# Attention scores for two heads at once, with new cost estimates in the kernel's own ordering

## The chip, the cores and the metric

The kernel runs on one core of a Trainium2 chip. The metric is the device time of one execution in microseconds; a figure without a unit is in microseconds too. Engines: TensorE (PE in the profile; PEld is its weight load), VectorE (DVE), ScalarE (ACT), GpSimd (POOL) and SyncE (SP), which issues the transfers. SBUF is the on-chip memory; PSUM is where TensorE writes, eight banks here used as eight tiles of 128 × 512 numbers.

## What is computed

A block of 256 tokens of width 1024 goes through two blocks in a row. The first has three mixers side by side (a short convolution, a stick-breaking attention with eight heads of 64, a retention), then attention to a memory, then a two-layer net. The second has a state-space mixer, a gated net with a short convolution, an attention with eight heads, and such a net again, with a layer norm behind each. The last attention is the place of the change. For each head its scores are the sum of a product over 128 features and one over 64 rotary features, whose key is shared by all heads:

```
scores = (einsum('bqhd,bkhd->bhqk', qn, k_nope)
          + einsum('bqhr,bkr->bhqk', qr, k_rope)) * scale
scores = where(key_idx <= q_idx, scores, -inf)
p = softmax(scores);  out = einsum('bhqk,bkhd->bqhd', p, v)
```

## The kernel before

All tokens stay on the chip; the weights (about 226 MB) are streamed in chunks of up to 1 MB. Products are made at nearly full float32 precision from pairs: every weight chunk is copied to a rounded high part `wh` (a cast on ScalarE) and a low part `wl` (the difference on VectorE), the activations likewise (`ah`, `al`), and each product is three passes on TensorE: high·high, high·low, low·high (`mm3`, line 685). Smaller products, such as those of the attention, are single products of float32 operands (`mm1`, line 963); in the trace each of these is two records.

The program is written by a planner while it is built. Wrappers around the engines (`Lane`, `Plan`, lines 272 to 435) add up for every instruction when it would start and end: `cost` (line 353) estimates its duration, `LATE` (line 25) the time from one engine's end to another's start, and the transfers have a rate of their own (line 412). Work that isn't one of the large products is a generator, a task (`spawn`, line 655), that yields where it has to wait for an engine. After each group of large products the planner calls `tick` (line 619), which steps every task whose operands are there by the estimates. `split_next` (line 594) decides when the next half chunk is cast and subtracted: if it is late against the estimated need (`need`, line 602: the estimated TensorE time of all chunks prepared, from `UNIT` in line 28 and `sums` in line 486, less the `work` done, line 688, and `skew`), or if the engine would otherwise be idle soon. So the estimates set no wait, but the order of the instructions in each engine's queue. Each engine works through its queue in order. The next weight transfer is issued when the second half of a chunk has been subtracted (`pump`, line 490).

Norms stand between the layers: a root-mean-square norm before the memory attention, the first net and the second block, a layer norm after each layer of the second block (`rms` line 875, `layernorm` line 902). Behind each, the result is transposed on TensorE and split into high and low.

The last attention (`attention`, line 1784): keys `knT`, queries `qnT` for 128 features, `krT` and `qrT` for the 64 rotary ones. `krT` has the shared key twice, in partitions 0 to 63 and 64 to 127, and `qrT` has an even head in the lower and an odd head in the upper 64 partitions. The queries come in two halves of four heads (line 1969). After each, the task `head` (line 1924) is started for each of the four heads. It takes one of four small PSUM tiles `sm`, makes 128 × 384 scores (the first 128 queries see 128 keys, the others 256): two products of 128 rows, two that add the mask, two of 64 rows. Then VectorE reduces the maxima, ScalarE takes the exponential with its sum, VectorE normalises, TensorE transposes, ScalarE copies, TensorE multiplies by the values `v`, and the result is split into `oT`. The output projection `ao` takes two heads per chunk and calls `before` (line 1977) to wait for those it needs.

In the first mixer the task `stick` (line 1005) handles two heads of 64 features together:

```
zs = yield from self.sm.wait(2)
rs = (slice(0, 64), slice(64, 128))
for z, r in zip(zs, rs):
    self.mm1(z[:, 0:256], kT[r, pair, 0:128], qT[r, pair, :], True)
for z, r in zip(zs, rs):
    self.mm1(z[:, 256:384], kT[r, pair, 128:256], qT[r, pair, 128:256], False)
```

Of the kernel before, what the change touches and what calls it, by code (L numbers as in the profile page):

```python
# [8 lines left out]
BF16 = mybir.dt.bfloat16  # L9
# [15 lines left out]
LATE = {("pe", "act"): 0.2, ("pe", "dve"): 0.2, ("act", "pe"): 0.22, ("dve", "pe"): 0.15, ("pool", "dve"): 0.06,  # L25
        ("pool", "act"): 0.06, ("pool", "pe"): 0.05, ("act", "pool"): 0.18, ("dve", "pool"): 0.16, ("act", "act"): 0.15,
        ("pe", "pe"): 0.0, ("dma", "act"): 0.95, ("dma", "dve"): 0.95, ("dma", "pe"): 0.95, ("dma", "pool"): 0.95}
UNIT = 6 / 2400
AHEAD = 1.0
FILL = 0.8  # L30
SOON = 0.0
# [258 lines left out]
class Plan:  # L290
# [62 lines left out]
    def cost(self, kind, name, out, ins, args, kw):  # L353
        n = 1
        for s, c in out.ap[1:]:
            n *= c
        psum = any(x.space == PSUM for x in ins)
        aps = sum(1 for x in ins[1:] if x.free_size() == 1)
        if kind == "pe":
            if name == "transpose":  # L360
                return 0.11
            if kw["rhs"].dtype == F32:
                m = kw["lhsT"].shape[-1]
                return 4 * max(n, m) / 2400 * (0.53 if m <= 64 else 1.0)
            return (n if n >= 256 or kw["rhs"].dtype == BF16 else 4 * n) / 2400
        if kind == "act":
            t = n / 1200 + (0.05 if psum else 0.093)
            if name in ("activation", "mul"):
                t += 0.093 * (len(ins) - 1) + (0.093 if "accum_out" in kw else 0)
            return t  # L370
        if kind == "dve":
            for x in ins[:1]:
                m = 1
                for s, c in x.ap[1:]:
                    m *= c
                n = max(n, m)
            if name == "reciprocal":
                return n / 160 + 0.07
            fast = name in ("tensor_copy", "tensor_scalar", "tensor_scalar_mul", "tensor_scalar_add") and not psum
            return n / (1920 if fast else 960) + 0.068 + (0.06 * aps if "scalar" in name else 0)  # L380
        if kind == "pool":
            return (0.3 + 0.16 * n if n < 3 else 0.6) if name == "tensor_tensor" else n / (280 if name == "tensor_copy" else 960) + 0.11
        return 0.0
# [88 lines left out]
class Kern:  # L472
    def __init__(self, nc, tc, a, dbg=None):
# [11 lines left out]
        self.work = self.skew = 0.0  # L485
        self.sums = np.concatenate([[0.0], np.cumsum([len(ks) * max(n, P) * UNIT for _, ks, _, n, _ in self.plan])])

# [197 lines left out]
    def mm3(self, outs, lhs, rhs, first, last, weights=True):  # L685
        passes = ((0, 0), (0, 1), (1, 0))
        if weights:
            self.work += sum(o.free_size() for o in outs) * 3 / 2400
        for q, (i, j) in enumerate(passes):
            for n, o in enumerate(outs):  # L690
                self.nc.tensor.matmul(o, lhsT=lhs[i], rhs=rhs[j][n] if isinstance(rhs[j], list) else rhs[j],
                                      start=first and q == 0, stop=last and q == 2, skip_group_check=True)
# [27 lines left out]
    def xstat(self, tag, nks, lhs, blocks, tail=0, after=None, before=None):  # L720
# [29 lines left out]
        if tail:  # L750
            chs = []
            for tau in range(2):
# [3 lines left out]
                for c in range(tail):  # L756
# [19 lines left out]
                    else:  # L776
                        self.skew = 0.0 if c == tail - 1 else self.skew + nk * chs[c][0].shape[2] * UNIT / 2
                    self.tick()
        return ps

    def wmixed(self, tag, act, nk, consumers, tasks=None):
# [4 lines left out]
        for tau in range(2):  # L786
            for c in range(n):
# [8 lines left out]
                if tau == 0:  # L796
                    self.skew = 0.0 if c == n - 1 else self.skew + nk * wh.shape[2] * UNIT / 2
                if tau:
# [637 lines left out]
    def ssd(self, h, act):  # L1436
# [259 lines left out]
        for tau in range(2):  # L1696
            got = [0]
            for i, (half, c) in enumerate(last):
                ch = so(half, c, (tau,), chs[i] if tau else None)
                chs.append(ch)  # L1700
                if tau == 0:
                    self.skew = 0.0 if i == 2 else self.skew + 2048 * UNIT / 2
                if i:
# [80 lines left out]
    def attention(self, h, act):  # L1784
# [4 lines left out]
        krT = pool.tile([P, S], F32, tag="krT", name="krT")  # L1789
        knT = pool.tile([P, 8, S], F32, tag="knT", name="knT")  # L1790
        qnT = pool.tile([P, 8, S], F32, tag="qnT", name="qnT")
        qrT = pool.tile([P, 4, S], F32, tag="qrT", name="qrT")
# [7 lines left out]
        for n, o in (("kvn", 0), ("qn", 256)):  # L1800
            b, w = ROWS[n]
# [89 lines left out]
        for tau in range(2):  # L1891
            for tag, nk, src, blocks in (("qr", 3, cq, [(0, 512)]), ("v", 2, ckv, [(0, 512), (512, D)])):
# [12 lines left out]
                else:  # L1905
                    self.skew = nk * wh.shape[2] * UNIT / 2 if tag == "qr" else 0.0
                if tag == "qr":
# [5 lines left out]
        def evac_to(dst, h0=0):  # L1913
            def run(pt, t):
                nc.scalar.copy(dst[:, h0 + t:h0 + t + 2, :], pt.rearrange("p (a b) -> p a b", a=2))
                self.free(pt)
                yield
            return run
# [2 lines left out]
        scale = 192 ** -0.5  # L1921
        obank = {}

        def head(i):
            sc = yield from self.sm.wait()
            r = slice(64 * (i % 2), 64 * (i % 2) + 64)
            self.mm1(sc[:, 0:128], qnT[:, i, 0:128], knT[:, i, 0:128], True)
            self.mm1(sc[:, 128:384], qnT[:, i, 128:256], knT[:, i, :], False)
            self.mm1(sc[:, 0:128], self.identb, self.maskb, False)
            self.mm1(sc[:, 256:384], self.identb, self.maskb, False)  # L1930
            self.mm1(sc[:, 0:128], qrT[r, i // 2, 0:128], krT[r, 0:128], False)
            self.mm1(sc[:, 128:384], qrT[r, i // 2, 128:256], krT[r, :], False)
            yield "dve"
            mx = self.tiny.tile([P, 2], F32, tag="mx", name="mx")
            nc.vector.tensor_reduce(mx[:, 0:1], sc[:, 0:128], axis=AX.X, op=MAX)
            nc.vector.tensor_reduce(mx[:, 1:2], sc[:, 128:384], axis=AX.X, op=MAX)
            nc.vector.tensor_scalar_mul(mx, mx, -scale)
            p = yield from ps_.wait()
            sm = self.tiny.tile([P, 2], F32, tag="sm", name="sm")
            cuts = ((0, 128), (128, 384))  # L1940
            for t, (b, e) in enumerate(cuts):
                nc.scalar.activation(p[:, b:e], sc[:, b:e], AF.Exp, bias=mx[:, t:t + 1], scale=scale, accum_out=sm[:, t:t + 1])
            self.sm.put(sc)
            yield "dve"
            nc.vector.reciprocal(sm, sm)
            for t, (b, e) in enumerate(cuts):
                nc.vector.tensor_scalar_mul(p[:, b:e], p[:, b:e], sm[:, t:t + 1])
            yield
            pt = yield from self.sm.wait()
            for b in range(0, 384, P):  # L1950
                nc.tensor.transpose(pt[:, b:b + P], p[:, b:b + P], self.ident)
            ps_.put(p)
            yield "act"
            w = yield from pT.wait()
            nc.scalar.copy(w, pt[:, :384])
            self.sm.put(pt)
            yield
            po = yield from self.sm.wait()
            c = slice(P * i, P * i + P)
            self.mm1(po[:, 0:256], v[:, 0, c], w[:, 0:256], True)  # L1960
            self.mm1(po[:, 128:256], v[:, 1, c], w[:, 256:384], False)
            pT.put(w)
            yield "act"
            yield from self.split((oT[0][:, i, :], oT[1][:, i, :]), po[:, :256])
            self.sm.put(po)

        hs = []
        for b in (0, 4):
            self.wstat("qn", cq, 3, evac_to(qnT, b))
            self.until(*g_qr, *g_v)  # L1970
            for i in range(b, b + 4):
                hs.append(self.spawn(head(i)))
                self.tick()
        g_, b_ = self.bcast("lmg1", self.gb, "gb"), self.bcast("lmb1", self.gb, "gb")
        act = self.new_act()

        def before(c):
            self.until(*hs[:2 * c + 2])
        ps = self.xstat("ao", [2] * 4, self.lhs(oT), [(0, 512), (512, 1024)], tail=TAIL["ao"], before=before,
                        after=lambda t, p, got: self.layernorm(t, h, g_, b_, act, p, got))  # L1980
        close()
# [106 lines left out]
```

## Time and profile before

| | |
|---|---|
| time, median of 3 runs | 1233.27 us (1233.09 to 1234.08) |
| the profiled execution, its own time | 1233.43 us |
| its span, first to last instruction | 1231.7 us |
| instructions | 20769 |
| VectorE, ScalarE, GpSimd busy | 852.7, 718.0, 53.2 us |

The span is what the trace covers; the time has 1.7 us more around it. The busy time of an engine counts a stretch once however many of its instructions overlap. Starts of neighbouring TensorE records lie closer together than their durations, since they are pipelined, so the pace of TensorE is read from start to start. Nearly all instructions come from one helper, so the line (L284) tells nothing, and the names of the tiles tell what an instruction is: `sm<-krT,qrT` is a product of the rotary key and query into a small PSUM tile.

### The profile page before, as it was taken

What the parts mean: (1) busy time and instruction counts of PE and PEld (TensorE: products, weight loads), DVE (VectorE), ACT (ScalarE), POOL (GpSimd) and SP (SyncE); (2) the same over time, 40 slices, a digit from 0 to 9 for tenths busy, and PEclk for the clock granted to TensorE, in tenths of its full rate; (3) what the DMA queues carried; (4) which work ended last, traced back from release to release, by engine and by line L of the source; (5) the groups of instructions that cost most, each with busy time, mean ns of one, the idle gap of its engine ahead of it and who ended that gap; (6) DMA issues with size and microseconds to landing.
All of it is one profiled execution on the core that took longest, in us unless ns stands there. A gap on an engine that the chain in (4) does not pass through costs nothing.

```text
span 1231.7 us, 20769 instructions
## 1 busy us (share of the span) xinstructions
PE 1214.2 (99%) x8468; PEld 1109.8 (90%) x8468; DVE 852.7 (69%) x1378; ACT 718.0 (58%) x1181; POOL 53.2 (4%) x85
## 2 busy tenths in 40 slices
PE   7999999999999999999999999999999999999997
PEld 5979999989989998888999898999988888999986
DVE  5666848677747765446887797888855866888853
ACT  5666546446536554345789765666643665666631
POOL 0011000000000000000111201000000000000000
PEclk9999999999999999999999999999999999999999
DMA  7643355546444556524556545555673442455560
GB/s 257 246 159 132 142 198 221 185 163 227 172 154 167 211 193 226 183 105 172 224 206 237 190 172 197 180 185 193 216 262 105 164 184 106 171 206 190 209 251 34
DMA packets 35425, 227.71 MB, mean 185 GB/s; under 512 B 4321, under 2 KB 4993, under 8 KB 11522
## 3 DMA queue, kind: packets, MB, share of 16 engines
q1 hardware_dynamic: 35330, 226.39, 51.1%
q8 instruction: 66, 1.08, 0.3%
q14 instruction: 29, 0.24, 0.1%
HBM read 225.27 MB, written 1.10 MB: 184 GB/s over the span
## 4 chain that ended last, share of the span: by engine, by line
PE 93%; DVE 3%; DMA 1%; ACT 1%; issue 0%; POOL 0%; SPq 0%; POOLq 0%; DVEq 0%; ACTq 0%
PE mm L284 84%; PE sm L284 9%; DMA wr<-wts 1%; DVE wl L284 1%; DVE x L284 1%; DVE tk L284 0%; POOL rs L284 0%; ACT wh L284 0%; SPq L284 0%; DVE dtw L284 0%; DVE ln L284 0%; DVE al L284 0%; ACT L284 0%; ACT tk L284 0%; POOLq L2084 0%
## 5 line engine op out<-in xcount | busy, mean ns | idle before, releaser
L284 DVE TENSOR_TENSOR wl<-wr,wh 128x1024 fp32r<-128x1024 f32 (+3 forms) x408 | 478.7, 1196 | 174.2 <-ACT wh L284 173.5
L284 ACT CAST wh<-wr 128x1024 fp32r<-128x1024 f32 (+3 forms) x408 | 403.9, 1030 | 160.4 <-PE mm L284 88.6
L284 PE MATMUL mm<-ah,wh 128*128 128x256 f32 (+1 forms) x1496 | 417.1, 279 | 0.0
L284 PE MATMUL mm<-ah,wl 128*128 128x256 f32 (+1 forms) x1496 | 413.6, 276 | 0.1
L284 PE MATMUL mm<-al,wh 128*128 128x256 f32 (+1 forms) x1496 | 413.4, 276 | 0.0
L284 PEld LDWEIGHTS mm<-ah,wh 128*128 128x128 f32 (+1 forms) x1496 | 280.2, 187 | 1.6 <-issue 1.1
L284 PEld LDWEIGHTS mm<-al,wh 128*128 128x128 f32 (+1 forms) x1496 | 280.3, 187 | 0.4
L284 PEld LDWEIGHTS mm<-ah,wl 128*128 128x128 f32 (+1 forms) x1496 | 280.2, 187 | 0.4 <-DVE wl L284 0.3
L284 DVE SCALAR_TENSOR_TENSOR r<-mm,pcol,r 128x255 f32<-128x255 f32 (+2 forms) x212 | 86.9, 474 | 35.1 <-ACT r L284 35.1
L284 PE MATMUL mm<-wl,ah 128*128 128x512 f32 (+3 forms) x320 | 106.1, 338 | 3.0 <-DVE wl L284 2.9
L284 PE MATMUL mm<-wh,ah 128*128 128x512 f32 (+3 forms) x320 | 108.7, 346 | 0.0
L284 PE MATMUL mm<-wh,al 128*128 128x512 f32 (+3 forms) x320 | 106.3, 338 | 0.5 <-DVE al L284 0.5
L284 PE MATMUL mm<-wh,gTh 128*128 128x512 f32 x304 | 96.2, 391 | 0.0
L284 PE MATMUL mm<-wl,gTh 128*128 128x512 f32 x304 | 95.6, 389 | 0.0
L284 PE MATMUL mm<-wh,gTl 128*128 128x512 f32 x304 | 95.5, 389 | 0.0
L284 ACT ACTIVATE r<-mm,pcol 128x256 f32<-128x256 f32 x96 | 48.9, 560 | 43.3 <-PE mm L284 43.3
L284 PEld LDWEIGHTS mm<-wl,ah 128*128 128x128 f32 x320 | 60.4, 190 | 10.0 <-DVE wl L284 4.6
L284 PEld LDWEIGHTS mm<-wh,gTl 128*128 128x128 f32 x304 | 57.1, 188 | 11.9
L284 PEld LDWEIGHTS mm<-wl,gTh 128*128 128x128 f32 x304 | 57.1, 188 | 11.8
L284 PEld LDWEIGHTS mm<-wh,gTh 128*128 128x128 f32 x304 | 56.7, 188 | 12.0 <-issue 0.6
L284 PEld LDWEIGHTS mm<-wh,al 128*128 128x128 f32 x320 | 60.2, 189 | 7.0 <-DVE al L284 1.2
L284 PEld LDWEIGHTS mm<-wh,ah 128*128 128x128 f32 x320 | 60.3, 189 | 6.5 <-issue 0.7
(296 smaller groups left out, 1576.6 us busy)
## 6 DMA issues: line engine op xcount, KB each, us to landing
wr<-wts SPq DMA_DIRECT2D x186, 1024.0 KB, 4.8
wr<-wts SPq DMA_DIRECT2D x11, 768.0 KB, 4.3
gb<-prow SPq DMA_DIRECT2D x12, 512.0 KB, 6.5
dec<-rows SPq DMA_DIRECT2D x8, 768.0 KB, 8.1
wr<-wts SPq DMA_DIRECT2D x4, 704.0 KB, 4.1
wr<-wts SPq DMA_DIRECT2D x4, 512.0 KB, 6.5
tk<-mem SPq DMA_DIRECT2D x2, 512.0 KB, 7.3
out<-x SPq DMA_DIRECT2D x4, 256.0 KB, 2.1
```

The source lines that it names most:

```text
L284: r = f(*args, **kw)
```

## The change

The scores move from `head` to a new task `scores`, which takes two PSUM tiles, makes the 128-row products of two heads, then the masks of both, then the 64-row products of the two heads in turn, and starts a `head` task for the softmax of each. `before` waits for the pairs first, then for the heads. Beside that, the estimates change: large products cost 17/16 of their columns at 2.4 per nanosecond (also in `UNIT` and `work`), ScalarE 1/1110 us per column and 0.1 us, VectorE 0.11 us in place of 0.068 us per instruction.

```diff
-UNIT = 6 / 2400
+UNIT = 6 * 17 / 16 / 2400
...
-            return (n if n >= 256 or kw["rhs"].dtype == BF16 else 4 * n) / 2400
+            return (n * 17 / 16 if n >= 256 else n if kw["rhs"].dtype == BF16 else 4 * n) / 2400
         if kind == "act":
-            t = n / 1200 + (0.05 if psum else 0.093)
+            t = n / 1110 + 0.1
...
-            return n / (1920 if fast else 960) + 0.068 + (0.06 * aps if "scalar" in name else 0)
+            return n / (1920 if fast else 960) + 0.11 + (0.06 * aps if "scalar" in name else 0)
...
-            self.work += sum(o.free_size() for o in outs) * 3 / 2400
+            self.work += sum(o.free_size() for o in outs) * 3 * 17 / 16 / 2400
...
-        def head(i):
-            sc = yield from self.sm.wait()
-            r = slice(64 * (i % 2), 64 * (i % 2) + 64)
-            self.mm1(sc[:, 0:128], qnT[:, i, 0:128], knT[:, i, 0:128], True)
-            self.mm1(sc[:, 128:384], qnT[:, i, 128:256], knT[:, i, :], False)
-            self.mm1(sc[:, 0:128], self.identb, self.maskb, False)
-            self.mm1(sc[:, 256:384], self.identb, self.maskb, False)
-            self.mm1(sc[:, 0:128], qrT[r, i // 2, 0:128], krT[r, 0:128], False)
-            self.mm1(sc[:, 128:384], qrT[r, i // 2, 128:256], krT[r, :], False)
+        def scores(j):
+
+            scs = yield from self.sm.wait(2)
+            for e, sc in enumerate(scs):
+                i = 2 * j + e
+                self.mm1(sc[:, 0:128], qnT[:, i, 0:128], knT[:, i, 0:128], True)
+                self.mm1(sc[:, 128:384], qnT[:, i, 128:256], knT[:, i, :], False)
+            for sc in scs:
+                self.mm1(sc[:, 0:128], self.identb, self.maskb, False)
+                self.mm1(sc[:, 256:384], self.identb, self.maskb, False)
+            for q, k, o in ((slice(0, 128), slice(0, 128), slice(0, 128)), (slice(128, 256), slice(0, 256), slice(128, 384))):
+                for e, sc in enumerate(scs):
+                    r = slice(64 * e, 64 * e + 64)
+                    self.mm1(sc[:, o], qrT[r, j, q], krT[r, k], False)
+            for e, sc in enumerate(scs):
+                hs[2 * j + e] = self.spawn(head(2 * j + e, sc))
+
+        def head(i, sc):
             yield "dve"
...
-        hs = []
+        hs, pairs = {}, []
...
-            for i in range(b, b + 4):
-                hs.append(self.spawn(head(i)))
+            for j in range(b // 2, b // 2 + 2):
+                pairs.append(self.spawn(scores(j)))
                 self.tick()
...
-            self.until(*hs[:2 * c + 2])
+            self.until(*pairs[:c + 1])
+            self.until(*[hs[i] for i in range(2 * c + 2)])
```

## Rows read from the trace of the kernel before

**Rows 1.** The page: its span and TensorE's busy time with its share.
```profile
span 1231.7 us, 20769 instructions
PE 1214.2 (99%) x8468; PEld 1109.8 (90%) x8468; DVE 852.7 (69%) x1378; ACT 718.0 (58%) x1181; POOL 53.2 (4%) x85
```

**Rows 2.** Busy time by stretch: its length, PE, PEld, DVE, ACT, POOL, clock, DMA.
```profile
0.00:20.00 20.00, 13.48 (x42) 8.61 (x43) 10.75 (x24) 10.39 (x17) 1.57 (x7) 1.00 0.83 288
20.00:1223.00 1203.00, 1200.01 (x8425) 1100.96 (x8424) 837.87 (x1345) 705.54 (x1158) 50.74 (x77) 1.00 0.51 184
...
540.00:580.00 40.00, 39.42 (x245) 34.28 (x243) 22.27 (x42) 20.07 (x35) 1.10 (x2) 1.00 0.29 107
...
940.00:960.00 20.00, 18.62 (x100) 15.63 (x99) 15.51 (x26) 10.36 (x20) 1.88 (x2) 1.00 0.39 132
...
1030.00:1060.00 30.00, 29.27 (x210) 26.76 (x209) 22.65 (x37) 18.33 (x31) 1.87 (x2) 1.00 0.34 117
...
1223.00:1231.70 8.70, 0.71 (x4) 0.25 (x2) 4.11 (x11) 2.02 (x6) 0.93 (x1) 0.83 0.17 61
```

**Rows 3.** Timeline of TensorE in the last attention: start, duration, instructions merged.
```profile
989.88 0.82 PE L284 MATMUL sm<-knT,qnT 128*128 128x128 f32 x4
990.53 0.28 PE L284 MATMUL sm<-maskb,identb 128*128 128x128 bf16 x2
990.74 0.92 PE L284 MATMUL sm<-krT,qrT 64*128 64x128 f32 x4
...
991.59 0.92 PE L284 MATMUL sm<-knT,qnT 128*128 128x128 f32 x4
992.35 0.28 PE L284 MATMUL sm<-maskb,identb 128*128 128x128 bf16 x2
992.55 0.92 PE L284 MATMUL sm<-krT,qrT 64*128 64x128 f32 x4
993.40 0.38 PE L284 MATMUL sm<-knT,qnT 128*128 128x128 f32 x1
...
997.03 0.44 PE L284 MATMUL sm<-cst,p 128*128 128x128 f32 x2
```

**Rows 4.** Busy time by stretch inside the last attention; columns as in rows 2.
```profile
989.88:997.03 7.15, 7.15 (x43) 4.83 (x41) 4.99 (x14) 4.44 (x12) 0.00 (x0) 1.00 0.40 147
997.03:1005.25 8.22, 8.22 (x66) 8.00 (x66) 6.02 (x17) 7.53 (x20) 0.00 (x0) 1.00 0.01 3
1005.25:1012.39 7.14, 7.14 (x42) 4.83 (x40) 5.84 (x16) 4.35 (x15) 0.00 (x0) 1.00 0.70 255
```

**Rows 5.** Timeline of TensorE in the first mixer, around one pair of heads.
```profile
47.87 0.92 PE L284 MATMUL sm<-qT,kT 64*128 64x256 f32 x8
48.72 0.50 PE L284 MATMUL mm<-wh,ah 128*128 128x512 f32 x1
```

**Rows 6.** Groups of TensorE instructions by form: count, busy us, mean ns, idle before.
```profile
L284 PE MATMUL sm<-maskb,identb 128*128 128x128 bf16 x16 | 2.2, 219 | 0.0
```

**Rows 7.** Timeline of VectorE: maxima and probabilities of the first head.
```profile
991.88 0.61 DVE L284 TENSOR_REDUCE mx<-sm 128x1 f32<-128x128 f32 x2
...
993.94 0.55 DVE L284 TENSOR_SCALAR p<-p,sm 128x128 f32<-128x128 f32 x2
```

**Rows 8.** Timeline of TensorE in the last net: first and last of twelve products.
```profile
1119.73 0.28 PE L284 MATMUL mm<-al,wh 128*128 128x256 f32 x1
...
1120.98 0.28 PE L284 MATMUL mm<-ah,wh 128*128 128x256 f32 x1
```

**Rows 9.** Groups by form: casts and differences of weight half chunks; columns as in rows 6.
```profile
L284 ACT CAST wh<-wr 128x1024 fp32r<-128x1024 f32 x376 | 380.0, 1050 | 154.3 <-PE mm L284 86.3 <-DMA wr<-wts 63.7 <-issue 2.6
...
L284 DVE TENSOR_TENSOR wl<-wr,wh 128x1024 fp32r<-128x1024 f32 x376 | 451.0, 1222 | 157.8 <-ACT wh L284 157.1
```

**Rows 10.** Waits of TensorE's weight loads: us in total, times, longest us.
```profile
PEld mm L284 <- DVE wl L284: 4.9, 7, 2.2
```

## The prediction

> **What bounds the kernel now.** I read the page's busy shares first: TensorE is busy for 1214.2 of the 1231.7 us span [rows 1]. Then the stretches: TensorE idles 6.5 us in the first 20 us (the first weights load), 8.0 us in the last 8.7 us (the closing layer norm), and 1203.0 − 1200.01 = 3.0 us in everything between. Of those 3.0 us, 2.7 lie in three stretches at the hand-over from one layer to the next: 0.58, 1.38 and 0.73 us [rows 2]. So between 20 and 1223 us the kernel is bound by how many nanoseconds of work TensorE is given, and a change helps in one of two ways: less TensorE time per product, or fewer of those 3.0 us. VectorE and ScalarE have room nearly everywhere; what they do costs only if TensorE must wait for it.
>
> **Part one: scores of two heads at once.** The timeline of TensorE shows how a head is paid for today [rows 3]. Its "knT,qnT" products (128 rows of the array) start at 989.88, its two mask products at 990.53, its "krT,qrT" products (64 rows) at 990.74, and the next head at 991.59: 0.65 + 0.21 + 0.85 = 1.71 us. The next head takes 0.76 + 0.20 + 0.85 = 1.81 us (991.59, 992.35, 992.55, 993.40). The 0.11 us more in its first term are what the way back from 64-row to 128-row products leaves behind. Four heads take 989.88 to 997.03 = 7.15 us, and the other four 7.14 us, with TensorE busy throughout [rows 4]; so time taken away here is time off the path, as long as work follows.
>
> Does taking turns pay? The kernel already does it in the first mixer: heads in pairs, one in the lower and one in the upper 64 rows, a 256-column product of each, then a 128-column product of each. Eight records of that run from 47.87 to 48.72, the start of the next product: 0.85 us for **two** heads [rows 5] (the other three pairs look the same). Here four records of **one** head take the same 0.85 us [rows 3]: the same column counts, the same number type, only one half of the array at work. The two halves then run beside each other. The new code has the same form: two heads, two PSUM tiles, two row halves, the products in turn (128 columns first, then 256). For each pair of heads:
> - krT: 2 × 0.85 becomes 0.85, which saves 0.85 us.
> - masks: 2 × 0.21 = 0.41 us now, each with its own change to 64 rows behind it. Two masks span 0.28 us and one takes 0.219 [rows 3, 6], so a further mask costs 0.06: four in a row cost 0.21 + 2 × 0.06 = 0.33. Saves about 0.09.
> - knT: the second head no longer follows 64-row products, 0.65 in place of 0.76. Saves 0.11.
>
> Together 1.05 us for a pair, **4.2 us** for four pairs; the 7.15 us should become about 5.05.
>
> What is late next? Both scores of a pair are complete only after 0.65 + 0.65 + 0.33 + 0.85 = 2.5 us, against 1.7 for a single first head: 0.8 us later. VectorE then reduces two heads (0.6 us each), so a first head's probabilities, ready at 993.94 + 0.55 = 994.49 today [rows 7], come some 0.8 to 1.5 us later, at 995.3 to 996.0, while TensorE is through its scores at 989.88 + 5.05 = 994.9 instead of 997.03, where it goes straight to the transposes [rows 3]. The cushion of 2.5 us is used up. What hides the gap is other TensorE work: in the first half the second half's query projection (36 products of 256 columns at 0.114 us [rows 8], 4.1 us), in the second half the output projection, whose first chunk needs only the first two heads. The ordering places transposes when it thinks the operand is there, so I book no wait; if the cover fails, the cost is the 0.4 to 1.1 us of the gap in each half, 2.2 us at most.
>
> Starting a head's softmax as a task of its own moves no operation to another engine and issues no DMA; waiting for two PSUM tiles instead of one costs nothing, since four heads already run back to back and so hold all four tiles. If only one is free, the output projection goes first. VectorE may sit in front of a reduction whose product isn't finished, with weight differences ("wl") queued behind it; it is busy for 4.99 of 7.15 us and 6.02 of the following 8.22 [rows 4], so that is covered.
>
> The Trainium skill, in "TensorEngine Tiling (Array Packing)", section "PSUM Bottleneck", speaks against such a change: faster products do not make reading PSUM faster, and that may become the limit. By it the gain of a half (2.1 us) would be lost wherever the softmax sets the pace, which is rival A. This trace can't yet show it: TensorE has no idle time there at the present pace.
>
> **Part two: the estimates.** They change no instruction, only the order in which each engine's queue is written. From the code: a 256-column product goes from 256/2400 = 0.1067 to 0.1133 us, +6.3%; a 1024-column cast from 0.946 to 1.0225, +8%; the 1024-column difference from 1.135 to 1.177, +4%. The trace has 0.114 us from product to product (11 steps in 1.25 us), and 1.050 and 1.222 us for the other two [rows 8, 9]. The PSUM reads of 256 columns rise more, by 0.04 to 0.07 us. So the three costs that carry nearly all of the plan move up nearly together, and their ratio, which decides the order, moves by 2 to 4%. Only the fixed margins and the modelled DMA rate stay, so weights seem to arrive a little earlier relative to TensorE than they did. With TensorE idle for just 3.0 us in the middle, the gain is bounded by **3.0 us**; the loss has no such bound, and its nearest rows are the hand-overs, of which the worst costs 1.38 us [rows 2]. I take 0, as the relative costs hardly move, and keep for the range −3.0 and +4.1: the three hand-overs that show no idle time, each rising to 1.38.
>
> Sum: 4.2 us off. The profiled execution took 1233.43 us, 0.16 above the median of 1233.27. 1233.43 − 4.2 = 1229.2, and 1229.1 against the median; I say **1229.2**.
>
> **Rivals.**
> A. *The softmax sets the pace* and half of the gain goes into waits: for it, the lost cushion; against it, the other work to fill in. 1233.3 − 2.1 = 1231.2, the same within what can be told. A difference of 0.2% (2.5 us) is about what a measurement of this kernel can tell from none.
> B. *The products don't overlap* for the new operands. Then only changes between row modes are saved: masks 0.09, knT 0.11, and one way in and out of 64 rows per pair. A head's knT and krT products have the same columns and take 0.65 and 0.85 us [rows 3], so that is 0.20. Together 0.40 × 4 = 1.6: 1233.3 − 1.6 = 1231.7. Against it stands the first mixer.
> C. *The new order delays a hand-over*. There are six between the first layer and the end (three root-mean-square norms and three layer norms with products behind them). There VectorE does the norm and the weight differences in one queue; with casts and differences both dearer in the plan, a difference can land behind the norm, and TensorE stands before it. The longest single wait of a TensorE weight load for "wl" is 2.2 us [rows 10]. If all six came to that, 13.2 us would stand in place of 3.0: 1229.2 + 10.2 = **1239.4**, slower. It outweighs the attention gain from (4.2 + 3.0)/6 = 1.2 us per hand-over, and shows as slower from 1.6 us. For it: 1.38 us is there already once. Against it: the others are under 0.75 or not to be seen.
> D. *The new order takes away the waits* on top of the pairs: most of the 3.0 us, 1226.6.
>
> **How the numbers follow.** Forecast 0.58, D 0.13, A 0.13, B 0.04, C in full 0.07, and 0.05 for C in part, which eats the gain. The range 1226.2 to 1233.3 takes in D at the lower end (1229.2 − 3.0), and A, B and the +4.1 us at the upper; C in full and whatever is better than D are left out. Faster: forecast, D and the part of A that keeps more than 2.5 us, 0.74. Same: the rest of A, B and C in part, 0.18. Slower: 0.08.
>
> **What the changed profile would show.** The pair's krT products as eight records in about 0.85 us, the scores of four heads in about 5.05 us instead of 7.15, fewer TensorE microseconds in that stretch and no new idle time behind it: part one right. If the eight records take 1.5 us, B. If the stretch from the first score to the output projection is no shorter though the scores are, A. If the rest of the span, outside the attention, differs by more than 3 us, my second part is wrong; the idle times at the hand-overs tell whether C or D.

## The result, and the profile after

The changed kernel takes 1257.14 us (median of 4 runs, 1255.62 to 1257.71), the kernel before 1233.32 in the same session: a ratio of 1.0187, 95% interval 1.0175 to 1.0200. It is slower by 24 us; the forecast was 1229.2, the range ended at 1233.3.

The page of the changed kernel: span, busy time, and the chain that ended last by engine.

```profile
span 1256.0 us, 20786 instructions
PE 1218.5 (97%) x8468; PEld 1111.6 (88%) x8468; DVE 853.4 (68%) x1378; ACT 719.3 (57%) x1178; POOL 48.8 (4%) x85
PE 87%; DVE 5%; DMA 3%; ACT 3%; POOL 1%; issue 1%; SPq 0%; POOLq 0%; DVEq 0%; ACTq 0%
```

Against [rows 1] the same 8468 products, VectorE and ScalarE within 1.3 us, and 24.3 us more span. No engine got more instructions to do: TensorE waits more. **The attention itself is right.** TensorE's timeline of the changed kernel there, for [rows 3]:

```profile
1008.35 1.47 PE L284 MATMUL sm<-knT,qnT 128*128 128x128 f32 x8
1009.65 0.39 PE L284 MATMUL sm<-maskb,identb 128*128 128x128 bf16 x4
1009.97 0.93 PE L284 MATMUL sm<-krT,qrT 64*128 64x128 f32 x8
1010.83 1.58 PE L284 MATMUL sm<-knT,qnT 128*128 128x128 f32 x8
...
1013.43 0.32 PE L284 MATMUL sm<-cst,p 128*128 128x128 f32 x1
```

The eight records of a pair's krT products take 1010.83 − 1009.97 = 0.86 us, the four masks 0.32, the scores of four heads 1013.43 − 1008.35 = 5.08 (7.15 before [rows 4]); the other four heads take 5.08 too. The Trainium skill, "TensorE: Matmul & The Clock Gate", section "Part 3: Packing small matmuls — row/col tiling", says that products in different row groups of the array run at the same time; these eight records agree.

Now the rest of the span. Waits of TensorE's weight loads, for [rows 10], then of its products (us in total, times, longest; the products' wait for `wl` was 2.9 us in 3 times before, the one for `r` wasn't there):

```profile
PEld mm L284 <- DVE wl L284: 17.3, 13, 3.4
```
```profile
PE mm L284 <- DVE wl L284: 13.3, 11, 3.2
...
PE sm L284 <- ACT r L284: 3.5, 1, 3.5
```

Stretches of the changed kernel, columns as in [rows 2] (the clock is the third number from the end):

```profile
20.00:1223.00 1203.00, 1181.91 (x8324) 1084.22 (x8323) 830.31 (x1332) 703.73 (x1148) 45.34 (x76) 0.99 0.51 183
685.00:692.00 7.00, 5.94 (x17) 4.88 (x18) 6.78 (x8) 4.30 (x8) 0.00 (x0) 0.51 0.52 186
...
960.00:980.00 20.00, 16.02 (x90) 14.03 (x89) 13.82 (x33) 8.28 (x18) 1.69 (x2) 1.00 0.52 174
1055.00:1067.00 12.00, 6.95 (x56) 6.34 (x54) 7.96 (x16) 4.98 (x10) 0.93 (x1) 1.00 0.43 166
1067.40:1074.30 6.90, 6.17 (x29) 6.17 (x30) 4.08 (x4) 1.81 (x2) 0.00 (x0) 0.51 0.58 202
```

TensorE's idle time between 20 and 1223 us is 1203.0 − 1181.9 = 21.1 us, where it was 3.0; with 1.9 us more at the two ends that makes 20.0 of the 24.3. The other 4.3 are busy time (1218.5 − 1214.2), although the pairs take 4.2 away: two stretches run at a granted clock of 0.51, with 5.94 and 6.17 us busy in them, and half of that, 6.1 us, is an estimate of what they add. That leaves 2.4 of the 8.5 us (4.3 + 4.2) unexplained. To place the loss I compared when both traces reach the same number of columns of the large products. The lag of the changed kernel grows like this (times of the kernel before):

| stretch before | what lies there | lag grows by, us |
|---|---|---|
| 0–662 | first block, start of the state-space layer | +3.7 |
| 662–720 | state-space layer | +7.0 |
| 720–801 | its end, hand-over to the gated net | +3.2 |
| 801–980 | net, hand-over to the attention | +4.5 |
| 980–1024 | the last attention | −5.4 |
| 1024–1049 | last hand-over: attention, layer norm, net | +9.9 |
| 1049–end | last net | +1.0 |

At the last hand-over ScalarE's and VectorE's timelines in the changed kernel read

```profile
1052.54 1.06 ACT L284 CAST wh<-wr 128x1024 fp32r<-128x1024 f32 x1
```
```profile
1055.24 1.22 DVE L284 TENSOR_TENSOR wl<-wr,wh 128x1024 fp32r<-128x1024 f32 x1
...
1058.48 0.74 DVE L284 SCALAR_TENSOR_TENSOR tk<-x,ln,gb 128x512 f32<-128x512 f32 x1
1059.68 1.42 DVE L284 SCALAR_TENSOR_TENSOR x<-tk,rs,gb 128x512 f32<-128x512 f32 x2 [0.45 <-POOL rs L284]
1061.01 1.22 DVE L284 TENSOR_TENSOR wl<-wr,wh 128x1024 fp32r<-128x1024 f32 x1
```

and TensorE's (in brackets the idle time before and who ended it)

```profile
1062.28 0.38 PE L284 MATMUL mm<-wl,ah 128*128 128x256 f32 x1 [3.16 <-DVE wl L284]
...
1064.09 0.28 PE L284 MATMUL mm<-wh,al 128*128 128x256 f32 x1
1064.21 0.28 PE L284 MATMUL mm<-wh,ah 128*128 128x256 f32 x1
...
1068.13 0.58 PE L284 MATMUL mm<-wl,ah 128*128 128x256 f32 x1 [2.90 <-DVE wl L284]
...
1068.73 0.42 PE L284 MATMUL mm<-wh,ah 128*128 128x256 f32 x1
1068.94 0.41 PE L284 MATMUL mm<-wl,ah 128*128 128x256 f32 x1
```

The cast of this half chunk ends at 1053.60, but its difference stands behind the whole layer norm on VectorE and starts at 1061.01; TensorE waits 3.16 us for it. ScalarE has its next casts behind a split (`ah`) that needs TensorE's transposes, so the following differences come late too: 2.90 us more. Then the granted clock falls to 0.51 for 1067.4 to 1074.3, and products start every 0.21 us, not every 0.12.

In the state-space layer it is the other way round: weight work stands ahead of what TensorE needs next. ScalarE reads out a product (1.02 us), makes two casts (1.98) and rounds an operand (0.84) before the step `r<-r` that TensorE waits for; the casts are the largest part. The tile of that step had been there since 673.56, when VectorE last wrote it. ScalarE's timeline there, and TensorE's:

```profile
681.85 1.02 ACT L284 ACTIVATE r<-mm,pcol 128x256 f32<-128x256 f32 x2
682.76 1.98 ACT L284 CAST wh<-wr 128x1024 fp32r<-128x1024 f32 x2
684.64 0.84 ACT L284 ACTIVATE yTh<-sm,pcol 128x256 fp32r<-128x256 f32 x2
685.37 1.68 ACT L284 ACTIVATE r<-r 128x512 f32<-128x512 f32 x3
```
```profile
686.06 1.11 PE L284 MATMUL sm<-cst,r 128*128 128x128 f32 x4 [3.53 <-ACT r L284]
```

### The profile page after: what moved, and what is told of

Its sections match the earlier page's. It is cut to its first block, busy times and chain, and to the rows that moved or that the text cites. A ratio compares the mean times of both kernels' runs of the same rounds, so it can differ in the third digit from the quotient of the medians.

```text
span 1256.0 us, 20786 instructions
## 1 busy us (share of the span) xinstructions
PE 1218.5 (97%) x8468; PEld 1111.6 (88%) x8468; DVE 853.4 (68%) x1378; ACT 719.3 (57%) x1178; POOL 48.8 (4%) x85
## 4 chain that ended last, share of the span: by engine, by line
PE 87%; DVE 5%; DMA 3%; ACT 3%; POOL 1%; issue 1%; SPq 0%; POOLq 0%; DVEq 0%; ACTq 0%
PE mm L284 78%; PE sm L284 9%; DVE wl L284 2%; DMA wr<-wts 2%; ACT wh L284 1%; DVE x L284 1%; POOL rs L284 1%; DVE r L284 0%; DVE tk L284 0%; DMA cst<-cst 0%; DVE al L284 0%; ACT tk L284 0%; ACT r L284 0%; DVE ln L284 0%; ACT ah L284 0%
```

## The experiments

**Which part of the change loses.** Four kernels, each with a part undone. The pairs alone, all estimates back:

```diff
-UNIT = 6 * 17 / 16 / 2400
+UNIT = 6 / 2400
...
-            t = n / 1110 + 0.1
+            t = n / 1200 + (0.05 if psum else 0.093)
...
-            return n / (1920 if fast else 960) + 0.11 + (0.06 * aps if "scalar" in name else 0)
+            return n / (1920 if fast else 960) + 0.068 + (0.06 * aps if "scalar" in name else 0)
```

> The pairs of heads alone, all estimates as before. Theory O (the loss is the new order that the estimates bring; the pairs work as forecast): 4.2 us under the kernel before, 1228 to 1230. Rival P (the pairs themselves upset the hand-over from the last attention to the last net, since they bring TensorE there earlier): the hand-over, which lost 9.9 us in the changed kernel, is lost here too, so 1233 to 1239. Both theories expect the scores of four heads in 5.1 us.

The estimates alone (`scores` and `head` as before):

> All new estimates, heads one at a time. Theory O: all the loss and none of the 4.2 us, 1259 to 1263, with the waits at the same places as in the changed kernel (state-space layer, each hand-over behind it). Rival P: no loss at the last hand-over, 1246 to 1252.

The pairs with TensorE's estimate alone, then with those of ScalarE and VectorE alone:

> Pairs and the estimate of TensorE alone; ScalarE and VectorE as before. If the estimates of ScalarE and VectorE carry the loss (theory O1): 1228 to 1236. If the slower TensorE in the plan carries it (theory O2: the plan sees less hurry for the weights): 1250 to 1258.

> Pairs and the estimates of ScalarE and VectorE alone; TensorE as before. Theory O1: the whole loss or more, 1255 to 1270, since the plan then holds the two engines to be slower and TensorE not. Theory O2: 1228 to 1236.

| kernel | us (runs) | ratio to before |
|---|---|---|
| before | 1234.06 (13) | |
| pairs alone | 1235.40 (10) | 1.0012 [1.0003, 1.0022] |
| estimates alone | 1261.18 (1) | |
| pairs, TensorE's estimate | 1244.85 (1) | |
| pairs, ScalarE's and VectorE's | 1258.98 (1) | |

The estimates alone cost 27 us, at the same places as in the whole change. Each half of them costs, and the losses don't add: 9.5 and 23.6 us on top of the pairs make 21.7 together. The 9.5 us lie between the two ranges that were expected for TensorE's estimate, so neither theory on it held. The halves lose at different places, too: by the lag TensorE's estimate loses 6.3 us before 300 us and 1.8 us in the state-space layer (662 to 720 us), the other two 0.8 and 10.5 us.

The pairs alone gain nothing, though their scores are as short. By the lag they gain 3.1 us in the attention and lose 5.0 at the last hand-over. TensorE's timeline and stretch there, pairs alone:

```profile
1044.38 0.39 PE L284 MATMUL mm<-wl,ah 128*128 128x256 f32 x1 [3.77 <-DVE wl L284]
...
1045.29 0.40 PE L284 MATMUL mm<-wl,ah 128*128 128x256 f32 x1
1045.49 0.42 PE L284 MATMUL mm<-wh,al 128*128 128x256 f32 x1
```
```profile
1045.30:1048.70 3.40, 3.40 (x19) 3.40 (x18) 1.89 (x4) 2.50 (x4) 0.00 (x0) 0.50 0.60 200
```

and VectorE's timeline of the pairs alone, in the attention and at that hand-over:

```profile
990.36 1.23 DVE L284 TENSOR_TENSOR wl<-wr,wh 128x1024 fp32r<-128x1024 f32 x1 [4.85 <-ACT wh L284]
993.22 0.62 DVE L284 TENSOR_REDUCE mx<-sm 128x1 f32<-128x128 f32 x2 [1.63 <-PE sm L284]
...
993.95 0.62 DVE L284 TENSOR_REDUCE mx<-sm 128x1 f32<-128x128 f32 x2
...
998.01 1.22 DVE L284 TENSOR_TENSOR wl<-wr,wh 128x1024 fp32r<-128x1024 f32 x1
```
```profile
1041.78 1.42 DVE L284 SCALAR_TENSOR_TENSOR x<-tk,rs,gb 128x512 f32<-128x512 f32 x2 [0.45 <-POOL rs L284]
1043.11 2.36 DVE L284 TENSOR_TENSOR wl<-wr,wh 128x1024 fp32r<-128x1024 f32 x2
```

The kernel before does both differences of that chunk in one go ahead of the first reduction, and at the hand-over writes two differences between the steps of the layer norm. VectorE before, at the two places:

```profile
989.61 2.36 DVE L284 TENSOR_TENSOR wl<-wr,wh 128x1024 fp32r<-128x1024 f32 x2 [4.88 <-ACT wh L284]
```
```profile
1038.20 1.21 DVE L284 TENSOR_TENSOR wl<-wr,wh 128x1024 fp32r<-128x1024 f32 x1
1039.33 0.68 DVE L284 SCALAR_TENSOR_TENSOR x<-x,mm 128x512 f32<-128x512 f32 x1
...
1039.94 1.22 DVE L284 TENSOR_TENSOR wl<-wr,wh 128x1024 fp32r<-128x1024 f32 x1
```

With the pairs, VectorE idles 1.63 us in front of a reduction, and the second difference of the chunk, ready to run, comes at 998.01, where the kernel before starts it at about 990.8. The second difference frees the buffer and lets the next transfer go, so the refill runs late.

**The planner's test for room.** `split_next` holds a difference back if it doesn't fit with 1.2 us of margin before the next step of a norm under way (`room`, line 598), unless it is late by the estimates. While no norm is under way there is no such limit. The edit changes the margin:

```diff
-            if t["dve"] + 1.2 < room or late:
+            if t["dve"] + 0.5 < room or late:
```

In the whole change, in the pairs alone and in the kernel before:

> The changed kernel, but a weight difference may go ahead of a norm's next step on VectorE if it delays it by up to 0.7 us (the 1.2 in the planner's test for room becomes 0.5). Theory R (the loss at the hand-overs is a weight difference held back behind the norm, because by the new estimate it no longer fits before it): most of the loss at the hand-overs goes, 1232 to 1242. Theory L (the order before is a point that many constants were fitted to, and any move off it loses): no better than the changed kernel, 1250 or more.

> Pairs of heads, old estimates, and the 1.2 in the test for room becomes 0.5. Theory R: the 5.0 us that the pairs lost at the last hand-over come back at least in part, 1228 to 1232. Theory L: one more move off the fitted point, 1235 to 1250.

> The kernel before with the 1.2 as 0.5 alone. Theory R: the three hand-overs that show 2.7 us of idle TensorE improve by 1 to 3 us, 1230 to 1233. Theory L: slower than before, 1236 or more.

Measured beside a kernel before of 1233.84 us: 1240.93 (1 run) for the whole change; 1238.43 for the pairs, ratio 1.0037 [1.0025, 1.0049]; 1233.08 for the kernel before, ratio 0.9993 [0.9983, 1.0002]. So that margin alone gives back 16 of the 24 us, nearly all that was lost in the state-space layer and at the earlier hand-overs; the last hand-over still loses 10.1 us by the lag.

In the state-space layer itself, though, the test can hold nothing back. The steps on GpSimd that belong to the norms between the layers (`rs` of 128x1) end ahead of it and start again behind it; the last and the next one in the changed kernel:

```profile
557.00 0.55 POOL L284 TENSOR_TENSOR rs<-ve,mhalf 128x1 f32<-128x1 f32 x1 [5.35 <-DVE ve L284]
...
769.44 1.00 POOL L284 TENSOR_TENSOR rs<-ln,mhalf 128x1 f32<-128x1 f32 x1 [14.40 <-DVE ln L284]
```

And the casts have a margin of their own, 1.0, which no run changed. So what the margin returns there must come through the order that the norms ahead of the layer leave behind; that path was not followed. It is hardly the luck of one order: in all seven kernels with 0.5, here and below, the lag grows by at most 0.7 us between 606 and 801 us, where it grows by 8.6 in the changed kernel.

The margin does nothing for the kernel before, and the pairs alone get worse: their loss at the last hand-over, which theory R had put down to the same test, is not cured by it.

**Is it the direction?** VectorE's estimate moved the other way by a fifth of the change, and, apart from that, the chunks' need raised by 1% without the work:

```diff
-            return n / (1920 if fast else 960) + 0.068 + (0.06 * aps if "scalar" in name else 0)
+            return n / (1920 if fast else 960) + 0.06 + (0.06 * aps if "scalar" in name else 0)
```
```diff
-UNIT = 6 / 2400
+UNIT = 6.06 / 2400
```

> The kernel before, with VectorE's fixed estimate moved the other way, from 0.068 to 0.06 us per instruction, by a fifth of the change's step. Theory R, and every theory in which longer estimates are what harms: 1231 to 1235, no loss. Theory L: a loss all the same, 1240 to 1255.

> The kernel before with only the estimated need for weights stretched by 1% (6.06 for 6 in the unit, a sixth of the change's step; the cost of a product and the work done stay). Theory L (any move off the fitted point loses): 1240 to 1260. A theory in which a step's size sets the loss: 1233 to 1237.

The first takes 1247.14 us (1 run): 8 ns less per VectorE instruction in the plan costs 13 us, in the state-space layer. ScalarE and TensorE there:

```profile
688.58 1.98 ACT L284 CAST wh<-wr 128x1024 fp32r<-128x1024 f32 x2
690.46 1.02 ACT L284 ACTIVATE r<-mm,pcol 128x256 f32<-128x256 f32 x2
691.37 0.51 ACT L284 ACTIVATE r<-r,rs 128x256 f32<-128x256 f32 x1
```
```profile
691.93 1.30 PE L284 MATMUL sm<-cst,r 128*128 128x128 f32 x4 [3.62 <-ACT r L284]
```

Two casts again, and the reading of a product, ahead of `r<-r,rs`, the operand that TensorE waits for. The second takes 1268.57 us (1 run), above both of the ranges that were expected; there every chunk seems less urgent the further the kernel is, and of 35 us of lag 23.5 come between 520 and 662 us. This is no small step, since the shift grows with the kernel, to about 12 us at its end (an estimate: 1% of the span). So the loss is not a matter of one direction: VectorE's estimate lowered loses 13 us, raised together with ScalarE's 23.6 us on top of the pairs. That every step away from the kernel before loses is not shown; its margin changed alone cost nothing. Whether the margin returns the first loss too was tried with both edits:

> The kernel before with VectorE's estimate lowered (0.06 us per instruction in place of 0.068) and the margin of the test for room 0.5 in place of 1.2. Theory R (the loss of 14 us that the lowered estimate brought is the test for room): most of it comes back, 1232 to 1236 us. Rival (another decision of the planner, such as when a task counts as ready, is what the lowered estimate upset): it stays at 1243 to 1250 us.

1235.57 us, ratio 1.0016 [1.0006, 1.0025]: of the 13 us, 2 are left. The margin returns this loss too, again in a layer without a norm under way.

**The weight work behind the reductions.** For the pairs' own loss the theory is that the two softmax tasks, started ahead of weight work that is ready, take VectorE's queue. The edit writes that work first, in `scores`:

```diff
+            while self.there():
+                self.copy()
+            while self.subs:
+                self.sub()
             for e, sc in enumerate(scs):
                 hs[2 * j + e] = self.spawn(head(2 * j + e, sc))
```

Alone on the pairs, on the pairs with the margin of 0.5, and on the whole change with that margin:

> Pairs of heads, old estimates; before the two softmax tasks of a pair are started, every cast whose weights are there and every weight difference that is pending is put into the queues ahead of them. Theory W (with the pairs VectorE gets the reductions of two heads ahead of a weight difference and idles before them, so the refill of the weight buffers falls some 7 us behind and is missing at the last hand-over): the 5.0 us lost there come back, 1228 to 1232. Rival S (the weights can't be prepared earlier anyhow, since a chunk needs a slot that only TensorE frees, so what TensorE gains it waits for): as the pairs alone, 1234 to 1237.

> As the run before with weights first, and the 1.2 in the test for room as 0.5. Theory W with R: 1226 to 1231, faster than both kernels. Rival S: 1234 or more.

> The changed kernel with weights first and 0.5 for 1.2, against 1240.9 us with the 0.5 alone. Theory W: most of the 10 us that the last hand-over still lost come back, 1230 to 1235. Rival S: 1239 to 1243.

| kernel | us (runs) | ratio to before |
|---|---|---|
| before | 1233.94 (11) | |
| pairs, weights first | 1230.06 (6) | 0.9971 [0.9960, 0.9982] |
| pairs, weights first, margin 0.5 | 1229.48 (5) | 0.9965 [0.9951, 0.9979] |
| whole change, weights first, margin 0.5 | 1232.21 (1) | |

At the last hand-over the loss by the lag is gone (+0.04 for 5.0). SyncE's transfer issues, pairs alone and then with the weights first:

```profile
985.54 18.29 SPq L284 DMA_DIRECT2D wr<-wts  x3
1003.88 2.02 SPq L284 DMA_DIRECT2D gb<-prow  x2
1022.55 0.33 SPq L284 DMA_DIRECT2D wr<-wts  x1
```
```profile
1006.74 17.11 SPq L284 DMA_DIRECT2D wr<-wts  x3
```

The fourth transfer of the attention carries the first chunk of the last net. A chunk is ready for TensorE when its last difference is done:

| us | pairs alone | weights first | before |
|---|---|---|---|
| the fourth transfer goes out | 1022.55 | 1006.74 | 1009.0 |
| its chunk is ready | 1036.4 | 1023.5 | 1025.2 |
| the next chunk is ready | 1045.5 | 1038.4 | 1041.2 |
| TensorE's first product of that next chunk | 1040.3 | 1039.6 | 1042.4 |

Only the pairs alone are too late, by the wait shown above. The last step of that chain is VectorE's queue again. ScalarE's casts of that next chunk, pairs alone:

```profile
1031.21 1.04 ACT L284 CAST wh<-wr 128x1024 fp32r<-128x1024 f32 x1
...
1035.44 1.06 ACT L284 CAST wh<-wr 128x1024 fp32r<-128x1024 f32 x1
```

They end at 1032.25 and 1036.50; the differences stand behind the layer norm and start at 1043.11, as in the changed kernel.

The pairs with the weights first, the second kernel of the table, beat the kernel before by 0.3%, and the changed one. The whole change with both edits takes 1232.21 us: with the weights first 8.7 us more come back than with the margin alone (1240.93; one run each), so the two edits together return the whole loss.

**One estimate alone with both edits.** The pairs, weights first, margin 0.5, and TensorE's estimate of the change:

> The pairs with the TensorE estimate of the change (17/16), weight work written ahead of the softmax tasks, and the margin 0.5. Theory (the estimate loses only by the test for room and by the weight work behind the reductions): 1228 to 1232 us, as the pairs with both edits and the old estimates. Rival (the TensorE estimate has a loss of its own, by the need that it shifts): 1235 to 1245 us.

1240.71 us, ratio 1.0059 [1.0043, 1.0074], where the same kernel with the old estimate takes 1229.48 and that with all the new ones 1232.21. The rival holds in this combination: TensorE's estimate costs 11.2 us that neither edit returns. It is not a price of that estimate alone, since the kernel with all the new ones contains it and loses nothing. Against the kernel with the old estimate, 3.6 us of lag are there by 606 us, and 5.8 us come in the attention, where its lag on the kernel before grows by 2.6 us and that of the other falls by 3.2; there TensorE waits for a head's probabilities:

```profile
1008.49 0.61 PE L284 MATMUL sm<-cst,p 128*128 128x128 f32 x3 [1.85 <-DVE p L284]
```

Behind this wait the granted clock is 0.51 from 1009.6 to 1013.1 us, with 3.5 us busy; half of that, 1.75 us, is an estimate of what it adds. Which decision of the planner puts the probabilities there stays open.

## Why the prediction was wrong

**Part one, TensorE's side: right.** 5.08 us for four heads against "about 5.05", krT 0.86 against 0.85, masks 0.32 against 0.33. Where the weights are kept in time, the gain comes out at 1233.94 × (1 − 0.9971) = 3.6 us [2.2, 4.9], for 4.2 in the sum; in that kernel TensorE waits 0.36 us for a `p` and 0.23 us for a `pT`, which may be the rest, though the interval is wider than that. Rival B is refuted. Among the waits of TensorE in the changed kernel none is for a `p`, so A is too: the softmax did not set the pace there. What the prediction took from the Trainium skill, "TensorEngine Tiling (Array Packing)", section "PSUM Bottleneck", that reading PSUM may become the limit, did not show in it; the 1.85 us above are the one wait for probabilities over 0.6 us in any run, under another order.

**Part one, what is late next: the step that failed first.** "VectorE may sit in front of a reduction whose product isn't finished, with weight differences ("wl") queued behind it; [...] so that is covered." With the pairs alone it does sit there (1.63 us). The busy share of VectorE in that stretch, on which I rested, says nothing about it: in a queue that is worked in order, what counts is what stands behind the waiting instruction. A difference stood there, behind it a transfer, and TensorE paid 5.0 us some 50 us later. With that work written first the 5.0 us are gone, which shows the cause.

**Part two: the step that failed most.** "I take 0, as the relative costs hardly move": the estimates alone cost 27 us. The mistake is the inference from small ratios to a small effect. The order comes from tests with fixed margins, of the kind "does this still fit before that". A small shift in the planned times can flip one, and a flip puts a whole difference or cast of 1.0 to 1.2 us in front of or behind something that TensorE needs. The lowered estimate shows how little is enough: 8 ns per instruction, 13 us. What the runs show in place of the 0: the margin of the test for room returns 16 of the 24 us (11 of 13 with the lowered estimate), and the weights written first return the rest. What stays open is why just these estimates upset the order, and how the margin reaches the state-space layer, where the test has nothing to hold back. I also bounded the loss by three hand-overs at 1.38 us, the worst row of the order that was to be replaced. Rows of one order don't bound what another order costs.

**Rival C** had the mechanism, a difference behind the norm and TensorE in front of it, and the sign. Its price, six times 2.2 us, was too low, and its place too narrow: the state-space layer, where casts stand in front of small steps, loses 7.0 us and was not in it. It also left out what the clock adds. I gave it 0.07 in full, since the other hand-overs showed under 0.75 us or nothing: once more rows of the old order. The text's own test, "if the rest of the span, outside the attention, differs by more than 3 us", fell at once: it is 29 us (24.0 + 5.4 of lag).

## What to carry to other kernels

Where a static order is computed from estimates, a change of the estimates is a new order, however near the ratios; time it by itself, and don't price it from waits of the order that it replaces. Before a task is started that reads a product not yet made, look at what is queued behind its first instruction, and write the work that is ready ahead of it; here two small loops turned no gain into 3.6 us. A shortage of weights shows where the buffers run dry, so follow the transfer issues back from a wait to the point where they first fall behind, and look at what the late piece stood behind in its engine's queue.

## What the runs showed of the hardware

Behind a wait of TensorE the clock can fall, and the lower clock then costs half as much again as the wait, or nearly as much as it. After 3.53 us of standing in the state-space layer the granted clock reads 0.51 over 685 to 692 us; after 3.16 and 2.90 us at the last hand-over, 0.51 over 6.9 us; with the pairs alone, after 3.77 us, 0.50 over 3.4 us. The level is the lower of two, 1.2 in place of 2.4 GHz: 256-column products start every 0.21 us, not every 0.12. By the half of the busy time, an estimate, the lower clock adds 3.0 us to the 3.5, 3.1 to the 6.1 and 1.7 to the 3.8; in the changed kernel that is 6 of the 24 us. The length of one wait doesn't decide it. The waits of 2.45 and 0.92 us around 970 us left the clock at 1.00, while a wait of 1.85 us in the last of the experiments had 0.51 behind it. With VectorE's lowered estimate two waits of 2.51 and 1.50 us, 2.5 us from the end of one to the end of the other, had 0.51 for 6.9 us behind the first. The Trainium skill, "TensorE: Matmul & The Clock Gate", section "What's actually happening", says that a gate sets the clock to one of two levels by how busy the engine was; the trace agrees with the levels and with the fall behind idle time. No term of the prediction held this.
